# An input projection by eight blocks of plain products, and by seven products of one Strassen level in two sweeps of 1024 tokens

## The chip, the cores and the metric

The kernel runs on one core of a Trainium2 chip. The metric is the device time of one execution in microseconds (us). Engines: TensorE (PE, matrix products; PEld is its weight load), VectorE (DVE), ScalarE (ACT), GpSimd (POOL), and SyncE (SP), which here issues the transfers between DRAM and the on-chip memory SBUF. Products are summed up in PSUM.

## The reference

One layer on x of 2048 tokens by 1024 features. The input is normalised and modulated, multiplied by one wide matrix, and the columns of that product go two ways:

```python
mod = c_act @ w_ada[layer] + b_ada[layer]
shift, scale, gate = jnp.split(mod, 3, axis=-1)
h = rmsnorm(x, norm_g[layer]) * (1.0 + scale[:, None, :]) + shift[:, None, :]
proj = h @ w_in[layer]
u_f, z_f, q, k, v, r, gf_low, gb_low = jnp.split(proj, pts, axis=-1)
y_f = fourier_mix(u_f, w_fmap[layer]) * jax.nn.silu(z_f)
y_g = gla_mix(q, k, v, gf_low, gb_low, w_af[layer], b_af[layer],
              w_ab[layer], b_ab[layer], gla_norm_g[layer]) * jax.nn.silu(r)
y = jnp.concatenate([y_f, y_g], axis=-1) @ w_out[layer]
x = x + gate[:, None, :] * y
...
return rmsnorm(x, final_g)
```

`u`, `z`, `v` and `r` have 1024 columns each, `q` and `k` 512, the two gate inputs 16 each. `fourier_mix` is a two-dimensional Fourier transform over tokens and channels in four groups of 256 channels. `gla_mix` is gated linear attention with four heads, one scan over the tokens forward and one backward.

## The kernel before

**Three passes.** A float32 value is split into a high part (rounded by ACT) and a low part (the remainder, by DVE or POOL; `split`, L45). `mm3` (L49) makes a product of two split values from three matmuls: high by high, high by low, low by high. All large products are made so.

**Start.** x comes transposed, with features on partitions. Shift and scale come from `w_ada` (L202 to L308), and the modulated input is kept in SBUF as `hT`, high and low, in four blocks of 512 tokens. The first block of `u` is multiplied while the input is still being made.

**Projection.** The columns are worked off in blocks. `proj_tok` (L335) has tokens on the output's partitions: four blocks of 256 columns for `u`, four of 264 for `v`, with 24 matmuls of 256 or 264 columns for each of 16 token tiles. `proj_col` (L345) has columns on the output's partitions: four blocks of 256 for `z`, two for `q`, two for `k`, four for `r`, with 24 matmuls of 512 tokens for each of eight pieces. Weights are loaded and split for each block (`load_w`, L112). Products go to PSUM tiles `pj` (three buffers). `u` and `z` stay in SBUF (`U`, `Z`, with the SiLU of `z` taken on the way out of PSUM); q, k, v and r go to DRAM.

**Fourier group.** `fourier` (L476) runs four times. `stage1` (L377) is a 16-point transform along the tokens on DVE, in place in `U`. Then come five steps over pairs of frequencies: twiddle factors (`tw`, L492 to L495) and split (`gp`) on DVE and ACT, matmuls `pq` (L504), split (`PQ`, L505), matmuls `mapA` (L520 to L527), and the products with `Z` (L533 to L538). `U`, `Z`, `T` (which holds `tw` and `cm`), `gp` and `PQ` have one buffer each. The program text is u, z, Fourier of group g, then two of the blocks of q, k and v (L565 to L588), with the scaling of the output weights between.

**Linear attention.** First the gates are transposed (`gtr`, L622). The backward sweep goes over 8 blocks of 256 tokens and two pairs of heads: 16 half-blocks, each with `prework` (L640 to L701: decay logits `lg`, a scan on DVE, the decayed `Q` and `K`), scores `sc`, outputs `ob`, and for each half of 128 tokens a transpose of the keys `ktr`, a split and the state update `upd` (L715 to L734). Three blocks of `r` come next in the program text (L775), the last one after the first forward step (L814). Then the forward sweep makes the same again with the other gates, and the output projection `po` (L911) runs beside it.

**Order.** The program text gives dependences. A scheduler that simulates a timeline while the program is built decides the order of instructions on each engine, and this order is then fixed. An engine works its row in order, so an instruction that waits holds up all behind it.

Of the kernel before, what the change touches and what calls it, by code (L numbers as in the profile page):

```python
# [21 lines left out]
P = 128  # L22
L = 2048
# [3 lines left out]
WC = 264  # L27
EPS = 1e-6
# [6 lines left out]
def hybrid_kernel(ctx, tc, i, out):  # L35
    nc = tc.nc
    V, S, G, T = nc.vector, nc.scalar, nc.gpsimd, nc.tensor

# [6 lines left out]
    def split(hi, lo, src):  # L45
        S.activation(hi, src, AF.Copy)  # L46
        V.tensor_tensor(lo, src, hi.bitcast(F32), ALU.subtract)  # L47
# [14 lines left out]
    yd_ = dram.tile([P, 16, 8, P], F32, name="yf_d")  # L62
    gd_ = dram.tile([P, L], F32, name="g_d")
# [4 lines left out]
    od_ = dram.tile([16, 2, P, 512], F32, name="ob_d")  # L68

# [6 lines left out]
    mhalf = cp.tile([P, 4], F32, name="mhalf")  # L76
# [24 lines left out]
    def load_w_half(src, cols, h, pool=None):  # L101
        if pool is None:
            stg = sp.tile([P, 4, WC], F32, tag="wst", name="wst", bufs=1)
        else:
            stg = pool.tile([P, 4, 256], F32, tag="wst0", name="wst", bufs=2)
        load(stg[:, :, 0:cols], src[:, 4 * h:4 * h + 4, :])
        hi = wp.tile([P, 4, WC], F32R, tag="whi", name="whi")
        lo = wp.tile([P, 4, WC], F32R, tag="wlo", name="wlo")
        split(hi[:, :, 0:cols], lo[:, :, 0:cols], stg[:, :, 0:cols])
        return hi, lo  # L110

    def load_w(src, cols):  # L112
        return [load_w_half(src, cols, h) for h in range(2)]

    def stage_tile():
        return sp.tile([P, 512], F32, tag="st", name="st")

    def evac_q(blk, dst, scale, c, b, ps):
        s = stage_tile()
        S.activation(s[:], ps, AF.Copy, scale=scale)  # L120
        store(dst[:, 2 * b:2 * b + 2, 2 * (blk % 2) + c, :], s[:].rearrange("p (a t) -> p a t", a=2))

# [1 line left out]
    hT = []  # L124
    with ExitStack() as st_stack:
        st = st_stack.enter_context(tc.tile_pool(name="start", bufs=2))
        ccol = st.tile([P, KT], F32, name="ccol", bufs=1)
        bcol = st.tile([P, KT, 2], F32, name="bcol", bufs=1)
        ng = st.tile([P, KT], F32, name="ng", bufs=1)
# [5 lines left out]
        S.activation(cact[:], ccol[:], AF.Silu)  # L135

        def new_h(b):
            hT.append(tuple(big_tile(f"hT_{n}{b}")[:].rearrange("p (k t) -> p k t", k=KT) for n in ("hi", "lo")))
            return hT[b]

        def modulate(hi, lo, x, k, n):
            g_, s_ = gs[:, k:k + 1], shift[:, k:k + 1]
            if n != 512 and k in (1, 3, 5, 7):
                V.tensor_scalar(x, x, g_, s_, ALU.mult, ALU.add)  # L144
                V.tensor_copy(hi, x)
                V.tensor_tensor(lo, x, hi.bitcast(F32), ALU.subtract)
                return
            S.activation(hi, x, AF.Identity, bias=s_, scale=g_)  # L148
            if n == 512:
                rest = st.tile([P, 512], F32, tag="rest", name="rest")  # L150
                S.activation(rest[:], hi.bitcast(F32), AF.Identity, bias=s_, scale=-1.0)
                V.scalar_tensor_tensor(lo, x, g_, rest[:], ALU.mult, ALU.add)
            else:
                V.tensor_scalar(x, x, g_, s_, ALU.mult, ALU.add)
                V.tensor_tensor(lo, x, hi.bitcast(F32), ALU.subtract)  # L155
# [16 lines left out]
        def load_x(hb):
            b, o = hb // 2, (hb % 2) * 256
            xb = st.tile([P, KT, 256], F32, tag="xb", name="xb", bufs=2)
            load(xb[:], i["xT"][b][:, :, o:o + 256])
            return xb

        def bcast_rstd(pair):
            rb = pf.tile([P, 256], F32, tag="pq", name="rb", bufs=2)
            for t in range(2):  # L180
                T.matmul(rb[:, t * P:(t + 1) * P], pair[t][:, 0:1].to_broadcast([P, P]), ident[:],
                         start=True, stop=True)
            return rb

        xt = up.tile([P, KT, 512], F32, tag="U", name="xt")
        ada = [big_f32(f"ada{j}") for j in range(4)]
        fin = big_f32("fold_in")
        fout = big_f32("fold_out")
        tabs = fin[:, 0:1024].rearrange("p (k w) -> p k w", k=2)
        wf = fin[:, 1024:3072].rearrange("p (g k d) -> p g k d", g=NG, k=2)  # L190

        def ada_block(j):
            return ada[j // 2][:, (j % 2) * 2048:(j % 2 + 1) * 2048].rearrange("p (k w) -> p k w", k=KT)

        wst0 = []

        def load_wst(h):
            stg = st.tile([P, 4, 256], F32, tag="wst0", name="wst", bufs=2)
            load(stg[:], i["w_in"][0][:, 4 * h:4 * h + 4, :])
            wst0.append(stg)  # L200

        for n in range(2):  # L202
            load(xt[:, 4 * n:4 * n + 4], i["xT"][0][:, 4 * n:4 * n + 4])
        load(tabs, i["chtab"].rearrange("k p w -> p k w"))
        load(wf[:, 0:2], i["w_fmap"][0:2].rearrange("g (k p) d -> p g k d", p=P))
        load(wf[:, 2:4], i["w_fmap"][2:4].rearrange("g (k p) d -> p g k d", p=P))
        load(ada_block(0), i["w_ada"][0])
# [71 lines left out]
        for j in range(KT):  # L279
# [20 lines left out]
            if j == 2:  # L300
                split_wst(1)
# [725 lines left out]
```

## Time and profile before

| what | value |
|---|---|
| time of three runs | 1719.95, 1710.4, 1714.62 us; median 1714.62 us |
| span of the profiled execution | 1708.0 us |
| median less that span (launch and end, and what runs differ by) | 6.6 us |
| busy in the span: PE, DVE, ACT, POOL | 1642.6, 932.0, 596.9, 247.0 us |
| moved by the DMA engines | 213.60 MB, 125 GB/s on average |
| read from and written to DRAM | 145.65 MB, 66.32 MB |

The page of the profile gives the span but not the profiled execution's own device time; for this the median stands in. "xN" is a count, and `out<-in` names the tiles that an instruction writes and reads. In the window view each engine has its busy time and, in brackets, its instructions. PEclk is the granted clock of PE, 1.00 being full speed. A matmul's listed duration is longer than the step from one to the next, as they are pipelined; the pace is read from the count in a window.

### The profile page before, as it was taken

How to read it: one execution, taken by the hardware profiler on the slowest of the kernel's cores; microseconds unless marked ns; L12 is line 12 of the kernel's file. 1: busy time of each engine (PE TensorE's matmuls, PEld its weight loads, DVE VectorE, ACT ScalarE, POOL GpSimd, SP SyncE). 2: the span in 40 equal slices, each digit the busy share in tenths (PEclk: the TensorE clock that was granted, in tenths of full speed). 3: DMA queues.
4: the chain of work that ended last, by engine and by line, in shares of the span. 5: the costliest groups of instructions: out<-in, count | busy, mean ns of one | idle time of the engine just before them, and what ended most of it. 6: DMA issues, size and time to landing. Idle time of an engine off the chain costs nothing.

```text
span 1708.0 us, 24827 instructions
## 1 busy us (share of the span) xinstructions
PE 1642.6 (96%) x9632; PEld 1445.5 (85%) x9632; DVE 932.0 (55%) x1930; ACT 596.9 (35%) x1188; POOL 247.0 (14%) x239
## 2 busy tenths in 40 slices
PE   5879999999999999999999999998899999999997
PEld 4868888988889899998999888887778888888886
DVE  5687242262421544215351588889766576576562
ACT  3632221112211222122221355455554454454442
POOL 2250000110011000000000021235312122131220
PEclk9889999999999999999999999999999999999999
DMA  9541113531134112701124455567734434444331
GB/s 363 181 136 46 44 62 94 194 101 50 62 120 158 36 55 69 248 26 38 45 75 134 143 176 182 167 222 217 249 105 157 139 100 145 129 129 134 110 109 50
DMA packets 143383, 213.60 MB, mean 125 GB/s; under 512 B 12833, under 2 KB 95009, under 8 KB 141857
## 3 DMA queue, kind: packets, MB, share of 16 engines
q1 hardware_dynamic: 143120, 211.76, 38.4%
q8 instruction: 75, 1.23, 0.3%
q14 instruction: 44, 0.35, 0.1%
q10 hardware_dynamic: 144, 0.26, 0.0%
HBM read 145.65 MB, written 66.32 MB: 124 GB/s over the span
## 4 chain that ended last, share of the span: by engine, by line
PE 68%; issue 12%; DVE 8%; DMA 7%; POOL 3%; ACT 2%; SPq 0%; POOLq 0%; DVEq 0%; ACTq 0%
PE pj L54 45%; PE po L911 7%; PE mapA L54 3%; PE pq L54 3%; PE upd L54 2%; PE ob L767 1%; DMA v_d<-st 1%; PE fold L235 1%; DMA y<-yf_d 1%; PE sc L711 1%; DVE xb L144 1%; POOL vl L742 1%; POOL rstd L854 1%; PE cps L285 1%; PE sc L712 1%
## 5 line engine op out<-in xcount | busy, mean ns | idle before, releaser
L54 PE MATMUL pj<-hT_hi,whi 128*128 128x512 f32 x768 | 304.6, 397 | 0.1
L54 PE MATMUL pj<-hT_lo,whi 128*128 128x512 f32 x768 | 304.5, 396 | 0.0
L54 PE MATMUL pj<-hT_hi,wlo 128*128 128x512 f32 x768 | 304.2, 397 | 0.0
L54 PE MATMUL pj<-whi,hT_lo 128*128 128x264 f32 (+1 forms) x992 | 282.6, 286 | 12.0 <-DVE hT_lo L155 8.6
L54 PE MATMUL pj<-whi,hT_hi 128*128 128x264 f32 (+1 forms) x992 | 283.2, 286 | 1.9 <-ACT hT_hi L148 1.4
L54 PE MATMUL pj<-wlo,hT_hi 128*128 128x264 f32 (+1 forms) x992 | 283.2, 286 | 1.2 <-DVE wlo L47 1.2
L742 POOL TENSOR_TENSOR vl<-v,vh 128x512 fp32r<-128x512 f32 x64 | 95.0, 1485 | 768.0 <-DMA qi<-q_d 421.2
L54 PEld LDWEIGHTS pj<-whi,hT_lo 128*128 128x128 f32 x992 | 188.8, 191 | 13.4 <-DVE hT_lo L155 9.4
L54 PEld LDWEIGHTS pj<-whi,hT_hi 128*128 128x128 f32 x992 | 189.3, 191 | 3.2 <-ACT hT_hi L148 1.6
L54 PEld LDWEIGHTS pj<-wlo,hT_hi 128*128 128x128 f32 x992 | 189.9, 191 | 1.7 <-DVE wlo L47 1.4
L54 PEld LDWEIGHTS pj<-hT_hi,whi 128*128 128x128 f32 x768 | 144.4, 188 | 31.6 <-ACT U L546 0.5
L54 PEld LDWEIGHTS pj<-hT_hi,wlo 128*128 128x128 f32 x768 | 144.2, 188 | 31.5
L54 PEld LDWEIGHTS pj<-hT_lo,whi 128*128 128x128 f32 x768 | 144.5, 188 | 30.2
L47 DVE TENSOR_TENSOR wlo<-wst,whi 128x1024 fp32r<-128x1024 f32 (+1 forms) x38 | 46.8, 1232 | 169.2 <-ACT whi L46 169.1
L911 PE MATMUL po<-wo_hi,fhi 128*128 128x512 f32 x256 | 104.2, 407 | 8.3 <-ACT fhi L46 3.6
L911 PE MATMUL po<-wo_hi,ghi 128*128 128x512 f32 x256 | 103.0, 402 | 0.0
L911 PE MATMUL po<-wo_lo,fhi 128*128 128x512 f32 x256 | 102.6, 401 | 0.0
L911 PE MATMUL po<-wo_lo,ghi 128*128 128x512 f32 x256 | 102.3, 399 | 0.0
L911 PE MATMUL po<-wo_hi,flo 128*128 128x512 f32 x256 | 101.6, 404 | 0.5 <-DVE flo L47 0.4
L47 DVE TENSOR_TENSOR PQ<-pq,PQ 128x512 fp32r<-128x512 f32 x36 | 24.9, 692 | 125.7 <-ACT PQ L46 125.7
L911 PE MATMUL po<-wo_hi,glo 128*128 128x512 f32 x256 | 83.4, 401 | 0.2 <-DVE glo L47 0.2
L471 POOL TENSOR_TENSOR wos<-wos,gater 128x1024 f32<-128x1024 f32 x8 | 20.5, 2580 | 385.6 <-issue 209.2
(216 smaller groups left out, 3097.7 us busy)
## 6 DMA issues: line engine op xcount, KB each, us to landing
wst<-in_w_in SPq DMA_DIRECT2D x32, 512.0 KB, 4.5
v<-v_d SPq DMA_DIRECT2D x64, 256.0 KB, 2.9
xr<-in_x SPq DMA_DIRECT2D x28, 512.0 KB, 4.1
v_d<-st SPq DMA_DIRECT2D x64, 132.0 KB, 1.8
ada<-in_w_ada SPq DMA_DIRECT2D x8, 1024.0 KB, 16.0
yf_d<-Z SPq DMA_DIRECT2D x8, 1024.0 KB, 7.0
wos<-in_w_out SPq DMA_DIRECT2D x8, 1024.0 KB, 5.6
wo_d<-wos SPq DMA_DIRECT2D x8, 1024.0 KB, 4.9
```

The source lines that it names most:

```text
L47: V.tensor_tensor(lo, src, hi.bitcast(F32), ALU.subtract)
L54: T.matmul(ps, a, b, start=(k == 0), stop=(k == n - 1))
L144: V.tensor_scalar(x, x, g_, s_, ALU.mult, ALU.add)
L235: T.matmul(ps[:, ct, :], tabs[:, k, w * 256 + ct * P:w * 256 + (ct + 1) * P], wf[:, g, k, :], start=(k == 0), stop=(k == 1))
L285: T.matmul(cps[:, w:w + 1], wa[:, k, w * P:(w + 1) * P], cact[:, k:k + 1], start=(k == 0), stop=(k == KT - 1))
L471: G.tensor_tensor(w[:, a], w[:, a], g[:], ALU.mult)
L711: T.matmul(ps[:, h, 0:128], ki[:, c0:c0 + P], qi[:, c0:c0 + P], start=True, stop=True)
L712: T.matmul(ps[:, h, 128:192], K[:, g, kof:kof + P], Q[:, g, qof:qof + 64], start=True, stop=True)
L742: G.tensor_tensor(vl[:], v[:], vh[:].bitcast(F32), ALU.subtract)
L767: T.matmul(ob[:, h, :], pre[2][:, 2 * h + s, 64:192], st_b[hp][:, h, :], start=True, stop=True)
L854: G.tensor_tensor(r[:, 0:n], r[:, 0:n], mhalf[:, 0:n], ALU.pow)
L911: T.matmul(ps[h][:], a, wo[j][q][:, cs], start=(first and a is yh and q == 0), stop=(last and a is yl))
```

## The change

The features and the tokens of one sweep, and the columns of a block, are each halved, and the product of two 2 by 2 block matrices is made by seven products of sums in place of eight (Strassen's method in Winograd's form, once). A sweep has 1024 tokens; the second half of the tokens goes first (m = 1), then the first half (m = 0).

- `a_tiles`, `a_prep` (new): seven sums of the input for each of four pairs of feature blocks, split into high and low. SBUF holds the set of one sweep (14 tiles of 2048 columns).
- `b_prep` (new, first sweep): for each block of columns the sums of the weights (POOL) and seven split pieces; each piece is stored to DRAM (`bc_`, `bt_`). `b_load` (new, second sweep) loads them from there. Pieces lie in tiles `B`, six buffers.
- `block_col`, `block_tok` (new): seven products each, gathered by DVE in SBUF tiles `p1`, `u2`, `u3`, and stored. A block of 256 columns by `block_col` has 84 matmuls of 512 tokens in a sweep; one of 512 or 528 columns by `block_tok` has 336 matmuls of 256 or 264 columns.
- `u` and `z` go through DRAM too (`u_d`, `z_d`); `load_u` and `load_z` fetch them, with the SiLU of `z` there. The scaling of `q` moves into `prework`.
- The first sweep is all of z, u, v, q, k, r for tokens 1024 to 2047. The second sweep's blocks stand between the Fourier groups in the program text.
- `lg`, `gtr` and `ktr` share one PSUM buffer (tag `lt`); before, `lg` had its own (tag `lg`), and `gtr` and `ktr` shared another (tag `tr`) with the forward sweep's `otr`.

```diff
+    def x_scale(x, rb, eng):
+        for kk in range(2):
+            eng.tensor_tensor(x[:, kk], x[:, kk], rb[:, 0], ALU.mult)
...
+    ORDER = (1, 6, 7, 5, 2, 4, 3)
+    LOW = {1: G, 6: V, 7: G, 5: V, 2: G, 4: V, 3: G}
...
+            if k == 6:
+                t[1] = tmp("t1")
+                G.tensor_tensor(t[1], q[0, 1], q[0, 0], ALU.subtract)
+                G.tensor_tensor(q[0, 1], q[1, 1], q[0, 1], ALU.subtract)
+                G.tensor_tensor(q[0, 0], q[1, 1], t[1], ALU.subtract)
+                return q[0, 0]
...
+                t = b_tile()
+                bv = b_view(t, np_, n)
+                split(bv[:, 0], bv[:, 1], source(k, h), LOW[k])
+                store(dst[len(srcs) * order.index(k) + h][:, 0:2 * np_ * n], t[:, 0:2 * np_ * n].bitcast(F32))
...
+    def block_col(A, B, emit):
+        t1, u2, u3 = (tmp_t(name)[:, 0:512] for name in ("p1", "u2", "u3"))
+        for k in ORDER:
+            ps = pj_tile()
+            for p in range(4):
+                for q, (bq, aq) in enumerate(PASSES):
+                    T.matmul(ps[:], B[k][0][:, bq, p, :], A[k][aq][:, p, :], start=(p == 0 and q == 0),
+                             stop=(p == 3 and q == 2))
+
+            def add(o, a):
+                V.tensor_tensor(o, a, ps[:], ALU.add)
+            if k == 1:
+                S.activation(t1, ps[:], AF.Copy)
+            elif k == 6:
+                add(u2, t1)
+            elif k == 7:
+                add(u3, u2)
...
+    for g in range(4):
+        do_z(1, A, g)
+    with tc.tile_pool(name="tokraw", bufs=1, side="right") as tk:
+        for j in range(2):
+            do_u(1, A, j)
+        for j in range(2):
+            do_v(1, A, j)
...
+    do_u(0, A, 0)
+    do_z(0, A, 0)
+    fourier(0, load_u(0), load_z(0))
+    acc = gate_sums()
+    do_z(0, A, 1)
+    do_q(0, A, 8, qd_)
+    gate_row(acc)
+    scale_out_weights([0, 2])
+    fourier(1, load_u(1), load_z(1))
+    scale_out_weights([4, 6, 8])
+    do_u(0, A, 1)
+    do_z(0, A, 2)
+    do_q(0, A, 9, qd_)
+    fourier(2, load_u(2), load_z(2))
+    scale_out_weights([10, 12, 14])
+    do_z(0, A, 3)
+    do_q(0, A, 10, kd_)
+    fourier(3, load_u(3), load_z(3))
+    do_q(0, A, 11, kd_)
+    for j in range(2):
+        do_v(0, A, j)
...
-        lg = pg.tile([P, 512], F32, tag="lg", name="lg")
+        lg = pg.tile([P, 512], F32, tag="lt", name="lg")
...
-        tp = pg.tile([P, 512], F32, tag="tr", name="ktr")
+        tp = pg.tile([P, 512], F32, tag="lt", name="ktr")
...
     for blk in range(12, 15):
-        do_r(blk)
+        do_r(0, A, blk)
```

The order on PE at one place of the Fourier group: before, in the middle of a pair of a late group (`pj` are the projection's matmuls).

```order
L54 MATMUL pj<-whi,hT_hi_603 128x264
L54 MATMUL pj<-wlo,hT_hi_603 128x264
L54 MATMUL mapA<-PQ,wm 128x256 x2
L54 MATMUL pj<-whi,hT_lo_604 128x264
L54 MATMUL pj<-whi,hT_hi_603 128x264
L54 MATMUL pj<-wlo,hT_hi_603 128x264
L54 MATMUL pj<-whi,hT_lo_604 128x264
L54 MATMUL mapA<-PQ,wm 128x256 x22
```

After, on PE in the third Fourier group's first pair, these rows stand (A and B are the new sums).

```order
L260 MATMUL pj<-A_hi,B 128x512 x2
L260 MATMUL pj<-A_lo,B 128x512
L260 MATMUL pj<-A_hi,B 128x512
L56 MATMUL pq<-thi,gp 128x256
L56 MATMUL pq<-tlo,gp 128x256
L56 MATMUL pq<-thi,gp 128x256 x2
L56 MATMUL pq<-tlo,gp 128x256
L56 MATMUL pq<-thi,gp 128x256
L56 MATMUL mapA<-PQ,wm 128x256 x2
L56 MATMUL pq<-thi,gp 128x256
L56 MATMUL pq<-tlo,gp 128x256
L56 MATMUL mapA<-PQ,wm 128x256 x22
```

Its third row is the program's last `pj` matmul: all blocks of the second sweep, `v` and `r` among them, stand ahead of it, and behind it the rows of the third and fourth Fourier groups follow each other with no `pj` between.

The order on PE in the backward sweep: before, at one half-block's logits.

```order
L54 MATMUL pj<-hT_lo_604,whi 128x512
L54 MATMUL pj<-hT_hi_603,wlo 128x512
L54 MATMUL pj<-hT_hi_603,whi 128x512
L651 MATMUL lg<-gt,wabb 128x256 x2
L767 MATMUL ob<-state_8088,Q 128x256 x2
L54 MATMUL upd<-vh,kth 128x256
L54 MATMUL upd<-vl,kth 128x256
L711 MATMUL sc<-qi,ki 128x128
L54 MATMUL upd<-vh,ktl 128x256
```

After, on PE from the second key transpose of the first half-block.

```order
L805 MATMUL ktr<-ident,K 128x128 x2
L850 MATMUL ob<-state_9037,Q 128x256 x2
L56 MATMUL upd<-vh,kth 128x256
L56 MATMUL upd<-vl,kth 128x256
L56 MATMUL upd<-vh,ktl 128x256
L56 MATMUL upd<-vh,kth 128x256
L56 MATMUL upd<-vl,kth 128x256
L56 MATMUL upd<-vh,ktl 128x256
L734 MATMUL lg<-gt,wabb 128x256 x2
L794 MATMUL sc<-qi,ki 128x128
```

Before, a half-block's logits stand ahead of the last update of the half-block before it, with `pj` around both; now they stand behind that update, and nothing of another half-block or of the projection lies between them and the scores that need them.

The order on DVE in the backward sweep: before, around the state updates (L733) of one half-block.

```order
L659 SCALAR_TENSOR_TENSOR pa<-lg,pa 128x512
L733 SCALAR_TENSOR_TENSOR state_8088<-state_8088,sm,upd 128x256 x2
L663 SCALAR_TENSOR_TENSOR pb<-reset,pa 128x512
L762 COPY sb<-sc 64x2x64
L47 TENSOR_TENSOR ktl<-ktr,kth 128x256
L733 SCALAR_TENSOR_TENSOR state_8088<-state_8088,sm,upd 128x256 x2
L670 COPY sm<-pb 128x8
```

After, around the same updates (L816 now).

```order
L816 SCALAR_TENSOR_TENSOR state_9037<-state_9037,sm,upd 128x256 x2
L49 TENSOR_TENSOR ktl<-ktr,kth 128x256
L816 SCALAR_TENSOR_TENSOR state_9037<-state_9037,sm,upd 128x256 x2
L719 TENSOR_TENSOR gt<-gf,gt 32x256
L742 SCALAR_TENSOR_TENSOR pa<-lg,pa 128x512
L746 SCALAR_TENSOR_TENSOR pb<-reset,pa 128x512
```

Before, the next half-block's prework (`pa`, the scan `pb`) goes on between the two updates; now it begins after the second.

More of the change, by code (lines that the diff above doesn't have):

```diff
@@ L75, in hybrid_kernel @@
     cact = cp.tile([P, KT], F32, name="cact")
[L76 removed]
+    mhalf = cp.tile([P, 8], F32, name="mhalf")
     gcol = cp.tile([P, KT], F32, name="gcol")
@@ L99, in pj_tile @@
         return pj.tile([P, 512], F32, tag="pj", name="pj")
[L101 to L110, printed above, removed]
@@ L112, in load_w @@
-    def load_w(src, cols):
-        return [load_w_half(src, cols, h) for h in range(2)]
-    def stage_tile():
[L116 to L124, printed above, removed]
-    with ExitStack() as st_stack:
[L126 to L129, printed above, removed]
+    def stage_tile():
+        return sp.tile([P, 2 * WC], F32, tag="st", name="st", bufs=4)
@@ new lines, in weights @@
+    def weights(kind, b, m):
+        if kind == "col":
+            if not m:
+                return b_load(1, 4, 128, bc_[b], ORDER)
+            raw = rw.tile([P, 2 * BW], F32, tag="raw", name="raw", bufs=1)
+            return b_prep([i["w_in"][b + 4]], 4, 128, bc_[b], [raw], ORDER)
+        n_ = 256 if b < 2 else WC
+        if not m:
+            return b_load(2, 2, n_, bt_[b], TOK_ORDER)
+        src = i["w_u"][b] if b < 2 else i["w_v"][b - 2]
+        raws = [tk.tile([P, 2 * BW], F32, tag="traw", name="traw", bufs=2) for _ in range(2)]
+        return b_prep([src[:, 4 * h:4 * h + 4, :] for h in range(2)], 2, n_, bt_[b], raws, TOK_ORDER)
@@ L172, in load_x @@
[L172 to L207, printed above, removed]
-        load_wst(0)
-        load(ada_block(1), i["w_ada"][1])
-        load(ada_block(2), i["w_ada"][2])
-        load(ada_block(3), i["w_ada"][3])
@@ new lines, in hybrid_kernel @@
+    xstack.close()
+    for g in range(4):
[5 more added lines that the diff above has]
+            do_v(1, A, j)
+    xp = xstack.enter_context(tc.tile_pool(name="xs2", bufs=1, side="right"))
+    xs = x_tiles(0)
+    rb = x_rstd(0, xs)
+    for p in range(4):
+        x_scale(xs[p], rb, G)
+    for blk in (8, 9):
+        do_q(1, A, blk, qd_)
+    for blk in (10, 11):
+        do_q(1, A, blk, kd_)
@@ L375, in hybrid_kernel @@
+    for blk in range(12, 16):
+        do_r(1, A, blk)
+    A = a_tiles()
+    for p in range(4):
+        a_prep(A, p, xs[p], LOW)
+    xstack.close()
+    prep.close()
     fconst = {}
+    up = fstack.enter_context(tc.tile_pool(name="u", bufs=1))
+    fp = fstack.enter_context(tc.tile_pool(name="f", bufs=1))
     def stage1(U, h):
@@ new lines, in load_z @@
+        for c in range(2):
+            load(Z[:, c], zd_[:, 2 * g + c])
+            S.activation(Z[:, c], Z[:, c], AF.Silu)
+        return Z
+    thi = fp.tile([P, 640], F32R, name="thi")
+    tlo = fp.tile([P, 640], F32R, name="tlo")
+    tw = fp.tile([P, 8, 3], F32, name="tw")
+    tabstg = fp.tile([P, 640], F32, tag="T", name="tabstg")
+    load(tabstg[:], i["seqtab"])
+    load(tw[:], i["tw"])
+    split(thi[:], tlo[:], tabstg[:])
+    fconst.update(thi=thi, tlo=tlo, tw=tw)
+    do_u(0, A, 0)
@@ L874, in tail_fwd @@
                                 ALU.mult)
-            tp = pg.tile([P, 4, P], F32, tag="tr", name="otr")
+            tp = pt.tile([P, 4, P], F32, tag="tr", name="otr")
             for c in range(4):
```

511 lines of the change are left out of this document (268 added, 243 removed).

## The prediction

> **What bounds the kernel now.** I read the page first (busy time, slices), then the groups by line, then windows by stage, then single pieces of the timeline.
>
> ```profile
> span 1708.0 us, 24827 instructions
> PE 1642.6 (96%) x9632; PEld 1445.5 (85%) x9632; DVE 932.0 (55%) x1930; ACT 596.9 (35%) x1188; POOL 247.0 (14%) x239
> PE   5879999999999999999999999998899999999997
> ```
>
> PE bounds: 96% busy, and its slices are full from the fourth on. How many matmuls the projection has is in the groups; their listed means (397 and 286 ns) overlap, so the pace comes from windows.
>
> ```profile
> L54 PE MATMUL pj<-hT_hi,whi 128*128 128x512 f32 x768 | 304.6, 397 | 0.1
> L54 PE MATMUL pj<-whi,hT_lo 128*128 128x264 f32 (+1 forms) x992 | 282.6, 286 | 12.0 <-DVE hT_lo L155 8.6
> ...
> 0.00:43.00 43.00, 23.90 (x103) 21.34 (x103) 25.35 (x42) 14.74 (x22) 12.24 (x13) 0.91 0.93 363
> 560.00:590.00 30.00, 30.00 (x131) 24.21 (x130) 20.22 (x72) 4.93 (x9) 0.00 (x0) 1.00 0.11 35
> 817.00:860.00 43.00, 43.00 (x358) 43.00 (x357) 17.55 (x37) 9.83 (x22) 0.00 (x0) 1.00 0.10 32
> 953.60:1179.90 226.30, 225.62 (x1223) 193.34 (x1222) 187.77 (x353) 117.31 (x229) 55.46 (x35) 1.00 0.59 185
> 1179.90:1708.00 528.10, 503.35 (x2590) 420.76 (x2588) 337.85 (x670) 245.94 (x521) 120.73 (x150) 0.99 0.41 131
> 1190.00:1210.00 20.00, 12.58 (x52) 10.24 (x53) 15.09 (x30) 13.80 (x24) 4.88 (x4) 0.83 0.92 308
> ```
>
> From 560 to 590 us PE runs `pj` of 512 alone: 30/131 = 0.23 us each. From 817 to 860 it runs matmuls of 256 and 264: 43/358 = 0.120 us. The fourth window is the backward sweep, the fifth the forward sweep, as these rows of their logits bound them; the first row is the gate transpose:
>
> ```profile
> 926.27 0.60 PE L622 MATMUL gtr<-ident,g 128*96 128x128 f32 x4
> ...
> 953.60 0.40 PE L651 MATMUL lg<-gt,wabb 128*128 128x256 f32 x2
> ...
> 1179.89 0.28 PE L651 MATMUL lg<-gt,wabf 128*128 128x256 f32 x1
> ```
>
> The same windows for tile `pj` alone show what keeps PE full in the backward sweep:
>
> ```profile
> 953.60:1179.90 226.30, 162.78 (x642) 117.67 (x641) 17.74 (x26) 0.00 (x0) 1.00 0.59 185
> 1179.90:1708.00 528.10, 4.61 (x18) 3.20 (x17) 1.33 (x2) 0.00 (x0) 0.99 0.41 131
> ```
>
> So 162.8 of its 226.3 us are projection, and the sweep's own products take 62.8. The sweep is a chain of dependent steps, and the projection is the work that PE does while the chain runs elsewhere. The Fourier groups stand the same.
>
> **The change part by part.** *Matmuls.* Before, 3x768 = 2304 of 512 and 3x992 + 96 (in the start) = 3072 of 264: 2304x0.23 + 3072x0.12 = 899 us. After, 12 blocks x 2 sweeps x 84 = 2016 and 4x2x336 = 2688: 786 us. Off: 112 us of PE time. That is the gain if PE stays full.
>
> *What covers what.* The order on PE says it doesn't: the last `pj` stands in the third Fourier group's first pair. Behind it come the rest of that group, all of the fourth, and the backward sweep, with nothing to fill PE. I price these three by their chains.
>
> A Fourier pair, from DVE, ACT and PE in the middle of a group:
>
> ```profile
> 141.52 1.23 DVE L389 TENSOR_TENSOR T<-U 128x1024 f32<-128x1024 f32 x1
> ...
> 165.39 0.30 DVE L436 COPY U<-T 128x256 f32<-128x256 f32 x1
> ...
> 829.19 0.41 PE L54 MATMUL mapA<-PQ,wm 128*128 128x256 f32 x2
> ...
> 838.26 0.69 DVE L47 TENSOR_TENSOR gp<-tw,gp 128x512 fp32r<-128x512 f32 x1 [0.70 <-ACT gp L46]
> ...
> 840.21 0.28 PE L54 MATMUL pq<-thi,gp 128*128 128x256 f32 x1
> ...
> 843.68 0.68 DVE L47 TENSOR_TENSOR gp<-tw,gp 128x512 fp32r<-128x512 f32 x1
> ...
> 845.89 0.28 PE L54 MATMUL pq<-thi,gp 128*128 128x256 f32 x1
> ...
> 848.88 0.69 DVE L47 TENSOR_TENSOR PQ<-pq,PQ 128x512 fp32r<-128x512 f32 x1 [4.52 <-ACT PQ L46]
> ```
>
> From `mapA` to the `gp` that the first `pq` needs: 838.95 - 829.19 = 9.8 us. From that `pq` to the second one's `gp`: 844.36 - 840.21 = 4.2. From there to `PQ`: 849.57 - 845.89 = 3.7. With hand-overs 18 us for a pair when PE waits for nothing else (22 as it ran). A group has three such pairs, one of the kind without twiddles (half, 9) and one with a single frequency, whose products `mapA` still have to be taken to `Z` at the end (19, an estimate): 82, I take 80. `stage1` takes 24 us (first two rows, with three other instructions between).
> Third group uncovered: **80**. Fourth: `U` has one buffer, so its 2 MB load starts when the third is through; 512 KB of `wst` take 4.5 us (below) and the load is wider, so 8; `stage1` 26; `scale_out_weights` stands on DVE inside it, 8; pairs 80: **122**. Gate transpose to logits as before, 953.6 - 926.3 = **27**.
>
> The backward sweep's chain:
>
> ```profile
> 956.61 0.58 ACT L654 ACTIVATE pa<-lg 128x512 f32<-128x512 f32 x1
> 957.21 1.28 ACT L641 ACT_TABLE_LOAD   x1
> ...
> 967.55 0.42 DVE L701 TENSOR_TENSOR K<-K,sm 128x256 f32<-128x256 f32 x1
> ...
> 972.26 0.38 ACT L46 ACTIVATE kth<-ktr 128x256 fp32r<-128x256 f32 x1
> ...
> 975.00 0.42 DVE L47 TENSOR_TENSOR ktl<-ktr,kth 128x256 fp32r<-128x256 f32 x1
> ...
> 981.90 1.02 PE L767 MATMUL ob<-state,Q 128*128 128x256 f32 x4
> ...
> L733 DVE SCALAR_TENSOR_TENSOR state<-state,sm,upd 128x256 f32<-128x256 f32 x112 | 48.6, 474 | 24.6 <-PE upd L54 24.4
> ```
>
> Logits to `K`: 967.97 - 956.61, less the 1.28 of a table load, is 10.0 us. Then a transpose (0.4), `kth` 0.38, `ktl` 0.42, six `upd` (6x0.12 and the pipeline, 0.8), two state updates 0.95, `ob` 0.5, six `upd` 0.8, two updates 0.95, next logits 0.4: 5.6, with eight hand-overs some 6.2. Before, one half-block's 10 us ran while the other's updates ran, and 16 took 226.3, 14.1 each. After, `lg` shares one PSUM buffer with `ktr`, stands on PE behind the last `upd`, and on DVE the prework stands behind the second update: nothing overlaps. 16 x 16.2 = **259**. Bounds: 240 (15 each), 290 (18).
>
> *First sweep.* The window 0:43 moved 363 GB/s. The start now needs 4 MB of x, 1.5 MB of Fourier maps, 8 MB of `w_ada` and 1 MB of weights: 14.5 MB, 40 us, and the normalisation stands ready at 43. Then POOL is in the way:
>
> ```profile
> L742 POOL TENSOR_TENSOR vl<-v,vh 128x512 fp32r<-128x512 f32 x64 | 95.0, 1485 | 768.0 <-DMA qi<-q_d 421.2 <-ACT vh L741 346.8
> L330 POOL TENSOR_TENSOR xb<-xb,rbs 128x1024 f32<-128x1024 f32 x10 | 25.9, 2612 | 10.1 <-DMA xb<-in_xT 9.6 <-issue 0.5
> ...
> 26.65 8.94 DVE L266 SCALAR_TENSOR_TENSOR acc<-ada,cact,acc 128x256 f32<-128x256 f32 x7
> ...
> 37.27 3.61 DVE L266 SCALAR_TENSOR_TENSOR acc<-ada,cact,acc 128x256 f32<-128x256 f32 x7
> ...
> wst<-in_w_in SPq DMA_DIRECT2D x32, 512.0 KB, 4.5
> ```
>
> Eight multiplications of 1024 (`x_scale`) are 8x2.61 = 21, sixteen low parts of 512 are 16x1.49 = 24; with 7 of waits the first block can run at 95, and its last six products take 17: **112** (95 to 135). The remaining sweep is 11x84x0.23 + 4x336x0.12 = 374. A block also stores 3.7 MB of weight pieces, loads 1 MB and stores 1 MB: 5.7 MB in 19.3 us, 295 GB/s, under the 363 above, so hidden, but near it. POOL has 4 sums and 4 low parts per block, 8x1.49 = 11.9 of 19.3 us: hidden. Stalls: `x_scale` of the second half stands on POOL between weight sums, 21 us of which 13 show; two raw tiles of `w_v`, `w_u` loaded at each of four changes (3 each), and some at the others (8): 33. **407** (385 to 490).
>
> DVE beside POOL is slowed: seven accumulations took 8.94 us while POOL multiplied, 3.61 alone. DVE has 7 sums and 3 low parts of 0.69 in a block, 6.9 of 19.3 us, and even 2.5 times that is hidden. The Trainium skill, SBUF — State Buffer, section "SBUF: two separate sides", says that a DVE instruction with two SBUF inputs and a GpSimd one lock each other out for the whole instruction; by it DVE plus POOL, 6.9 + 11.9 = 18.8 of 19.3 us, would be nearly full in the first sweep; a slip there belongs to rival B.
>
> *Second sweep to the last `pj`.* 1008x0.23 + 1344x0.12 = 393, and 432 Fourier matmuls of the first two groups, 52; their order leaves about 16 us of `pj` between the steps of a pair against the 18 that its chain takes, 2 in each of six pairs: 12. **457** (440 to 480). Loads of pieces (3.7 MB a block, none to split) are hidden as above.
>
> *Forward sweep.* Its `pj` were 4.6 us: 528 - 5, less some waits that the separate `otr` buffer frees, **520** (500 to 530).
>
> *The clock.* With PE 63% busy (1190 to 1210) 0.83 was granted. On the uncovered chains PE's own steps are 2x26 (Fourier) and 16x3 us, 100; at 0.83 they cost **20** more.
>
> Sum: 112 + 407 + 457 + 80 + 122 + 27 + 259 + 20 + 520 = 2004 us. The median of before is 6.6 over its span; so **2010 us**, 17% slower: 112 us saved on PE, and some 410 in which it now waits where it did not (about 150 in two Fourier groups, 202 less their own 52; 215 in the backward sweep, 279 less 63; 27 at the gates; the rest in the start and the stalls).
>
> **The rivals.**
> A, the chains overlap down to what DVE has to do. Its rows in a Fourier pair:
>
> ```profile
> 834.93 0.63 DVE L537 TENSOR_TENSOR Z<-Z,cm 128x256 f32<-128x256 f32 x1
> 835.47 0.65 DVE L538 TENSOR_TENSOR Z<-Z,cm 128x256 f32<-128x256 f32 x1
> 836.16 0.35 DVE L492 TENSOR_SCALAR tw<-U,tw 128x256 f32<-128x256 f32 x1
> 836.69 0.48 DVE L494 SCALAR_TENSOR_TENSOR tw<-U,tw 128x256 f32<-128x256 f32 x1
> ```
>
> Two each of four `tw` (1.7), `gp` and `PQ` (1.4) and four steps on `cm` and `Z` (2.1, the first two 0.4 each) are 10.3 us by durations that overlap a little: 9.5 a pair, 41 a group; with `stage1` and 10 for load and scaling the fourth has 75. The backward sweep has 187.77 - 17.74 = 170. Without a clock loss: 112+407+457+41+75+27+181+515+7 = 1822. For: engines queue ahead, and before, the two half-blocks did overlap. Against: the order on DVE, and the shared buffer.
> B, the first sweep is fed too slowly (295 GB/s asked, or DVE and POOL locking each other out): 16 blocks x 5 us = 80 more, 2090. For: 0.93 DMA share at 363 GB/s. Against: large pieces.
> C, PE goes cold on the chains. At half clock its 100 us cost 100, not 20: 2090. The Trainium skill, TensorE: Matmul & The Clock Gate, Part 1, says that the granted clock falls to half after an idle window of about 3.4 us; the row with 0.83 at 63% busy agrees in direction only, so the row, not the rule, has the larger chance.
> D, faster: the second sweep's projection still covers the chains, PE stays the bound: 1715 - 112 = 1603, plus some start. It decides at a total of some 200 us for all stretches without `pj` (80+122+27+259 = 488 here): below that, the saved 112 win. DVE alone has 41+75+170 = 286 in them, which speaks against.
>
> **How the numbers follow.** Forecast 0.60; A 0.14; B 0.12; C 0.10; D 0.04, of it 0.03 faster and 0.01 the same. The range leaves out A and D (0.18): low from the low ends (95+385+440+70+100+20+240+500+7 = 1857), so 1860; high 2130, over B and C together with some of the high ends. A difference of 0.5% is about what a measurement of this kernel can tell from none: faster 0.03, same 0.01, slower 0.96.
>
> **What would show it.** Last `pj` near 976 us; PE busy about 75%; no `pj` behind it; logits 16 us apart, not 14; PE's granted clock under 1.00 in these stretches. It is wrong if PE's slices stay at 9 behind the last `pj`, if the half-blocks come every 11 us (A), if the first sweep ends beyond 600 us (B), or if the last `pj` stands later than 1100 us.

## The result, and the profile after

The changed kernel takes 2036.92 us in the median of four runs (2035.31 to 2042.27), against 1714.95 us of the kernel before on the same chip: 1.190 times as long (95% interval 1.186 to 1.194). The forecast was 2010 us in a range of 1860 to 2130.

Page of the changed kernel's profile, span, busy times and slices:

```profile
span 2035.8 us, 25168 instructions
...
PE 1654.2 (81%) x8984; PEld 1429.6 (70%) x8984; DVE 1118.3 (55%) x2196; ACT 624.8 (31%) x1182; POOL 490.3 (24%) x406
...
PE   6379999799899999999952543645558999999998
...
PEclk8679999899999999999965666666768999999999
```

PE has 648 matmuls fewer and is busy for longer, since a matmul at a low granted clock counts for longer (one of 512 columns 0.80 us at 0.50 in place of 0.40, below). The slices show two places: the second, with 3, and ten from the twenty-first on, where PE's digit falls to 2 to 6 and its clock to 0.5 to 0.7. Before, these eleven were 8 or 9.

Window view of the changed kernel by stage (PE, PEld, DVE, ACT, POOL busy with their instructions, granted clock, DMA share, GB/s). In order: start and first block of z; rest of z; u and v; q, k and r of the first sweep; second sweep to the last `pj`; the rest of the Fourier groups; gate transposes; backward sweep; forward sweep:

```profile
0.00:140.00 140.00, 70.79 (x308) 59.40 (x309) 83.93 (x114) 49.21 (x77) 66.51 (x42) 0.73 0.51 189
140.00:200.00 60.00, 56.99 (x244) 45.22 (x243) 21.93 (x30) 13.96 (x24) 38.05 (x30) 1.00 0.75 282
200.00:361.00 161.00, 160.16 (x1341) 159.95 (x1340) 60.92 (x113) 41.78 (x73) 72.64 (x56) 1.00 0.79 294
361.00:558.00 197.00, 176.36 (x763) 140.52 (x762) 85.58 (x104) 61.18 (x100) 125.86 (x84) 0.95 0.70 253
558.00:1014.00 456.00, 448.09 (x2741) 399.67 (x2742) 270.52 (x589) 64.31 (x105) 29.61 (x13) 0.99 0.81 284
1014.00:1202.00 188.00, 93.41 (x427) 81.28 (x425) 120.06 (x251) 41.19 (x65) 15.32 (x6) 0.63 0.30 107
1202.00:1225.00 23.00, 3.48 (x17) 2.07 (x16) 4.29 (x18) 3.06 (x6) 0.00 (x0) 0.57 0.57 171
1225.00:1519.00 294.00, 148.25 (x616) 122.16 (x616) 151.37 (x326) 114.77 (x227) 41.78 (x33) 0.65 0.33 107
1519.00:2036.00 517.00, 496.70 (x2536) 419.32 (x2536) 319.68 (x656) 235.35 (x506) 100.57 (x144) 0.97 0.38 123
```

Two bounds need care. The first sweep's last product ends at 551 us, so the last 7 us of the fourth window (some 60 matmuls) belong to the second sweep. The last bound is the first `po` matmul (1519); the forward sweep's first logits, which bound the windows of the prediction and most of those below (not e3's and e11's), come at 1535.9. By them the backward sweep takes 311 us and the forward sweep 500.

The second sweep to the last `pj` runs at PE's pace. Behind it come 188 + 23 + 294 = 505 us in which nothing bounds by its busy time: DVE, the busiest, has 276 of them. Such a stretch is a chain. The list of what PE waited for names its links (total, times, longest):

```profile
PE sc L794 <- DVE ki L763: 118.3, 16, 10.6
PE pq L56 <- ACT gp L48: 81.0, 14, 41.1
PE pj L260 <- POOL A_lo L49: 28.3, 4, 19.0
PE pj L260 <- ACT B L48: 25.4, 7, 13.8
```

The first is the prework of each of the 16 half-blocks. The second has two parts, as PE's timeline of the Fourier groups shows:

```profile
1049.66 5.75 PE L56 MATMUL mapA<-PQ,wm 128*128 128x256 f32 x24 [0.69 <-ACT PQ L48]
...
1068.29 5.06 PE L56 MATMUL mapA<-PQ,wm 128*128 128x256 f32 x24 [0.69 <-ACT PQ L48]
...
1128.34 0.58 PE L56 MATMUL pq<-thi,gp 128*128 128x256 f32 x1 [41.13 <-ACT gp L48]
```

One wait of 41 us is `stage1` of the fourth group, with the scaling of output weights between; the other 40 us are the twiddled values of the pairs, which come 18.6 us apart (first two rows). The last two entries of the list are mostly the start. PE's timeline in the backward sweep, logits and the scores behind them (last bracket: wait before it):

```profile
1247.20 0.40 PE L734 MATMUL lg<-gt,wabb 128*128 128x256 f32 x2
1255.15 0.79 PE L794 MATMUL sc<-qi,ki 128*128 128x128 f32 x2 [7.55 <-DVE ki L763]
...
1265.05 0.40 PE L734 MATMUL lg<-gt,wabb 128*128 128x256 f32 x2
1272.84 0.80 PE L794 MATMUL sc<-qi,ki 128*128 128x128 f32 x2 [7.39 <-DVE ki L763]
...
1284.86 0.40 PE L734 MATMUL lg<-gt,wabb 128*128 128x256 f32 x2
```

From logits to logits 17.9 and 19.8 us; over all 16, from 1225.2 to the last at 1510.8, 19.0. Each time PE stands still for 7.5 us for the keys of the very half-block whose logits it has just made.

### The profile page after: what moved, and what is told of

Same layout as the page of the kernel before. It is cut to its first block, busy times and chain, and to the rows that moved or that the text cites. A ratio compares the mean times of both kernels' runs of the same rounds, so it can differ in the third digit from the quotient of the medians.

```text
span 2035.8 us, 25168 instructions
## 1 busy us (share of the span) xinstructions
PE 1654.2 (81%) x8984; PEld 1429.6 (70%) x8984; DVE 1118.3 (55%) x2196; ACT 624.8 (31%) x1182; POOL 490.3 (24%) x406
## 5 line engine op out<-in xcount | busy, mean ns | idle before, releaser
L260 PE MATMUL pj<-A_hi,B 128*128 128x512 f32 x1344 | 438.0, 405 | 47.3 <-ACT B L48 25.4
L260 PEld LDWEIGHTS pj<-A_hi,B 128*128 128x128 f32 x1344 | 257.8, 193 | 115.5 <-ACT B L48 29.5
L303 PE MATMUL pj<-B,A_hi 128*128 128x256 f32 (+1 forms) x1792 | 326.3, 283 | 4.0 <-DVE u L264 2.4
L260 PE MATMUL pj<-A_lo,B 128*128 128x512 f32 x672 | 271.6, 404 | 28.3 <-POOL A_lo L49 28.3
L303 PEld LDWEIGHTS pj<-B,A_hi 128*128 128x128 f32 x1792 | 278.4, 189 | 4.9 <-DVE u L264 2.6
L303 PE MATMUL pj<-B,A_lo 128*128 128x256 f32 (+1 forms) x896 | 253.4, 283 | 0.8 <-DVE A_lo L49 0.8
L794 PE MATMUL sc<-qi,ki 128*128 128x128 f32 x256 | 72.6, 375 | 124.7 <-DVE ki L763 118.3
L260 PEld LDWEIGHTS pj<-A_lo,B 128*128 128x128 f32 x672 | 129.5, 193 | 60.8 <-POOL A_lo L49 30.7
L303 PEld LDWEIGHTS pj<-B,A_lo 128*128 128x128 f32 x896 | 169.1, 189 | 1.0 <-DVE A_lo L49 1.0
L56 PE MATMUL mapA<-PQ,wm 128*128 128x256 f32 x480 | 80.0, 327 | 7.9 <-ACT PQ L48 6.2
```

The source lines that it names most:

```text
L56: T.matmul(ps, a, b, start=(k == 0), stop=(k == n - 1))
L260: T.matmul(ps[:], B[k][0][:, bq, p, :], A[k][aq][:, p, :], start=(p == 0 and q == 0), stop=(p == 3 and q == 2))
L303: T.matmul(ps[:, j, :], A[k][aq][:, p, t * P:(t + 1) * P], B[k][p // 2][:, bq, p % 2, :], start=(p == 0 and q == 0), stop=(p == 3 and q == 2))
L794: T.matmul(ps[:, h, 0:128], ki[:, c0:c0 + P], qi[:, c0:c0 + P], start=True, stop=True)
```

## The experiments

Each was timed in several runs beside the kernel before, which took 1710 to 1715 us. "Ratio" is to that kernel, with its 95% interval.

| run | us | ratio |
|---|---|---|
| changed kernel | 2036.9 | 1.190 (1.186 to 1.194) |
| e1: before, r moved ahead | 1806.2 | 1.055 (1.051 to 1.058) |
| e8: before, shared buffer | 1841.5 | 1.073 (1.069 to 1.077) |
| e11: before, both of these | 1941.8 | 1.136 (1.133 to 1.138) |
| e2: changed, logits' own buffer | 1911.6 | 1.116 (1.113 to 1.119) |
| e3: changed, r late | 2033.7 | 1.187 (1.183 to 1.190) |
| e4: changed, PE kept busy | 2000.2 | 1.167 (1.163 to 1.170) |
| e5: changed, start on VectorE and spread | 2034.1 | 1.186 (1.182 to 1.189) |
| e6: e2, e3 and e5 together | 1923.2 | 1.121 (1.118 to 1.124) |
| e7: e6 and Fourier buffers | 1812.3 | 1.057 (1.053 to 1.061) |
| e9: e2 and Fourier buffers | 1812.5 | 1.058 (1.056 to 1.061) |
| e10: e9 and the start on VectorE | 1790.2 | 1.045 (1.043 to 1.046) |

**The cover alone (e1).** In the kernel before, with plain products, the four blocks of r join the first Fourier group's list and leave the backward sweep:

```diff
-    others = [[lambda: do_q(8, qd_, P ** -0.5), lambda: do_q(9, qd_, P ** -0.5)],
+    others = [[lambda: do_q(8, qd_, P ** -0.5), lambda: do_q(9, qd_, P ** -0.5)] +
+              [lambda blk=blk: do_r(blk) for blk in range(12, 16)],
...
-    for blk in range(12, 15):
-        do_r(blk)
...
-    do_r(15)
```

> The kernel before, plain products, with its four blocks of r moved from the backward sweep into the first Fourier group; nothing of the change is in it. Theory (cover): time is lost where chains run with no projection beside them, whatever the products cost. Then 4x192x0.23 = 177 us are spent earlier, and the backward sweep, which took 226 us with them, takes some 200 without: 1715 + 177 - 26 = 1866 us (1835 to 1910). Rival (the loss lies in the new products themselves, their sums and trips through DRAM): moving plain products about costs nothing, 1715 within 15.

It took 1806, 93 us more: slower without any Strassen product, but less than the 151 that I expected. The window of its backward sweep:

```profile
1124.00:1290.00 166.00, 117.53 (x628) 97.81 (x629) 154.29 (x328) 113.07 (x231) 45.70 (x32) 0.86 0.60 191
```

The sweep takes 166 us, not 200, and DVE is busy for 154 of them: without cover the half-blocks still overlap and VectorE sets the pace, 9.6 us each. Before, the same took 14.1, because the projection was there to be done. So lost cover does not explain 294 us in the changed kernel.

**The shared buffer (e2, e8, e11).** e2 gives the logits back their own PSUM buffer in the changed kernel, with the layout of before:

```diff
-    pj = ph1.enter_context(tc.tile_pool(name="pj", bufs=4, space=PSUM, side="right"))
+    pj = ph1.enter_context(tc.tile_pool(name="pj", bufs=3, space=PSUM, side="right"))
...
-            ps = pg.tile([P, 512], F32, tag="lt", name="gtr")
+            ps = pg.tile([P, 512], F32, tag="tr", name="gtr")
...
-        lg = pg.tile([P, 512], F32, tag="lt", name="lg")
+        lg = pg.tile([P, 512], F32, tag="lg", name="lg")
...
-        tp = pg.tile([P, 512], F32, tag="lt", name="ktr")
+        tp = pg.tile([P, 512], F32, tag="tr", name="ktr")
...
-            tp = pt.tile([P, 4, P], F32, tag="tr", name="otr")
+            tp = pg.tile([P, 4, P], F32, tag="tr", name="otr")
```

> The changed kernel with the PSUM layout of before: the logits have a buffer of their own, the key transposes share theirs with the forward sweep's transposes, three projection buffers in place of four. Theory (half-blocks of the backward sweep can't overlap because logits and key transposes share a buffer): they overlap again, 14 us each, 294 us become 225 to 240, and the time falls from 2037 to about 1975. Rival (each half-block's chain, lengthened by the low clock, sets the pace, whatever buffer it has): within 15 of 2037.

125 us less, twice what the theory gave. Its windows, Fourier rest, gates and backward sweep:

```profile
1019.00:1207.00 188.00, 90.48 (x428) 78.53 (x427) 120.24 (x251) 41.38 (x66) 15.31 (x6) 0.65 0.31 108
1207.00:1230.00 23.00, 4.12 (x17) 2.59 (x18) 4.23 (x17) 2.90 (x6) 0.00 (x0) 0.53 0.59 176
1230.00:1390.00 160.00, 112.47 (x631) 91.94 (x631) 149.12 (x323) 109.88 (x225) 44.65 (x31) 0.90 0.60 194
```

The other two stretches are as they were; the backward sweep falls from 311 to 160 by the same bounds, with the same work on DVE. Logits now start before the half-block ahead of them is through, as PE's timeline of this run shows, five in a row 7.6 to 11.8 us apart:

```profile
1244.73 0.78 PE L734 MATMUL lg<-gt,wabb 128*128 128x256 f32 x2
...
1252.35 0.48 PE L734 MATMUL lg<-gt,wabb 128*128 128x256 f32 x2
...
1264.14 0.50 PE L734 MATMUL lg<-gt,wabb 128*128 128x256 f32 x2 [1.21 <-DVE pa L742]
...
1274.56 0.58 PE L734 MATMUL lg<-gt,wabb 128*128 128x256 f32 x2
...
1284.39 0.58 PE L734 MATMUL lg<-gt,wabb 128*128 128x256 f32 x2
```

e8 is the mirror: the kernel before with `tag="lt"` for `lg`, `gtr` and `ktr`.

> The kernel before with one edit of the change: logits, gate and key transposes share one PSUM buffer. Its order on PE puts 23 us of projection into each of the first seven half-blocks and none into the last eight. Theory (the shared buffer makes every half-block one chain): seven of 23 + 4 us and nine of 16.5 are 338 in place of 226, and what is no longer spread must be paid: 1715 becomes 1770 to 1830. Rival (the chain of a half-block hides beside the projection): within 8 of 1715.

126 us more, in a kernel with plain products and all of its cover; that is above the 1830 at which the expectation ended. Its order packs the projection into the first half of the sweep (655 `pj` matmuls there, 6 in the second half), and the windows of the two halves show it:

```profile
953.50:1139.00 185.50, 183.71 (x901) 153.26 (x900) 96.79 (x170) 59.86 (x107) 31.49 (x19) 1.00 0.47 146
1139.00:1335.00 196.00, 110.35 (x449) 90.70 (x447) 104.19 (x211) 77.38 (x148) 31.49 (x22) 0.67 0.37 117
```

In the first half PE is full, in the second it has only the sweep's own matmuls at a clock of 0.67, and the 196 us are chain. e11 puts both edits into the kernel before.

> The kernel before, plain products, with both edits that were made to it singly: r moved into the first Fourier group, and logits and key transposes in one PSUM buffer. No Strassen product, no second sweep, no trip of weights through DRAM is in it. Theory (the shared buffer makes an uncovered half-block one chain of 18 to 19 us, as in the changed kernel): the backward sweep takes about 294 in place of 166, 1806 + 128 = 1934 (1915 to 1950). Rival (its length in the changed kernel comes from something else of the change, such as traffic or GpSimd's and VectorE's load): within 20 of 1806.

1942, as the theory said. Its backward sweep:

```profile
1124.00:1418.00 294.00, 147.37 (x618) 121.61 (x618) 151.87 (x327) 115.79 (x230) 42.70 (x33) 0.67 0.34 107
```

294 us to the first `po` with 618 matmuls at 0.67, where the changed kernel has 294 with 616 at 0.65; in both the logits come 19.0 us apart. Nothing of Strassen's method is in this run, so its traffic and its sums have no part in the sweep's length.

**The clock (e4).** Behind the logits of each half-block 36 matmuls into a spare buffer that nobody reads, and the blocks of r ahead of the sweep in the text, where their order on PE already was:

```diff
-            T.matmul(lg[:, h * 256:(h + 1) * 256], wab[d][:, c0:c0 + P], gt[:], start=True, stop=True)
+            mm = T.matmul(lg[:, h * 256:(h + 1) * 256], wab[d][:, c0:c0 + P], gt[:], start=True, stop=True)
+        if d == 1:
+            with tc.issue_after(mm.ins):
+                spare = pj_tile()
+                for n in range(36):
+                    T.matmul(spare[:], wab[1][:, 0:P], wab[1][:], start=(n == 0), stop=(n == 35))
```

> The changed kernel with 36 extra matmuls of 512 behind each half-block's logits in the backward sweep, into a spare buffer that nobody reads: 8.3 us at full clock in a wait of 7.5 to 10.6, and 17 x 8.3 = 141 us of PE work more. Theory (the low granted clock, 0.65 there, lengthens the steps of PE on the chain): the clock goes up to 0.9 or more and the backward sweep falls from 294 to about 260, the time to about 2003. Rival (the chain's other engines set the pace, and the clock costs only what PE would wait anyway): within 15 of 2037. If the extra work itself delays the scores: slower, 2050 or more.

37 us less for more work. Its backward sweep:

```profile
1228.00:1493.00 265.00, 234.88 (x1220) 196.88 (x1221) 154.46 (x337) 114.37 (x231) 42.70 (x33) 0.97 0.38 119
```

The granted clock is 0.97 in place of 0.65, and to the forward sweep's first logits the sweep takes 265 in place of 311. Half-blocks come every 16.7 us in place of 19.0; sixteen times 2.3 are the 37. With e2 this gives the parts: the chain at nearly full clock some 265, a low clock some 40 on top, and overlap would take 100 off (e2's 160).

**Cover moved within the changed kernel (e3, e6).** e3 makes `block_col` a generator that stops after each product, and takes two products of r behind each half-block's logits:

```diff
+        if d == 1:
+            with tc.issue_after(mm.ins):
+                next(rest, None)
+                next(rest, None)
...
-    for blk in range(12, 15):
-        do_r(0, A, blk)
+    for _ in rest:
+        pass
...
-    do_r(0, A, 15)
```

> The changed kernel with the second sweep's four blocks of r (28 products, 77 us) taken out from between the Fourier groups and put two by two behind the logits of the backward sweep's half-blocks, 5.5 us into a wait of 7.5 to 10.6. Theory (cover): they fill idle time there, the second sweep ends 50 to 77 us earlier, the backward sweep stays at 294 or gets shorter by a faster clock: 1935 to 1990. Rival (they were needed as cover between the Fourier groups, where as much waiting opens): within 15 of 2037.

No gain that can be told from none. Its windows, from the end of v to the gates, and the backward sweep:

```profile
940.00:1165.00 225.00, 96.02 (x432) 84.08 (x432) 135.40 (x322) 36.76 (x61) 9.37 (x4) 0.60 0.32 111
1187.00:1530.00 343.00, 247.71 (x1006) 201.14 (x1007) 196.27 (x376) 136.92 (x256) 63.15 (x41) 0.73 0.52 166
```

The gates start at 1166 in place of 1203, 37 us sooner for 77 us of matmuls taken away: the rest reappears as waiting. The backward sweep then takes up the 37: its half-blocks are 21.4 us apart in place of 19.0. The theory counted the products as free in a wait of 7.5 us, and they weren't; whether by the low clock or by their 28 additions on DVE this run doesn't separate. e6 tried the same with the logits' own buffer and e5's start.

> The changed kernel with three of the edits together: logits in a buffer of their own, r put late into the backward sweep, the start's multiplication on VectorE. From 1911 (logits alone) less 30 (start); r late saved 39 us ahead of the gates and gave them back in the backward sweep. Theory (given back because each half-block was one chain of 19 us): with overlapping half-blocks of 9.5 us the two products cost little, 1911 - 30 - 39 + 20 = 1862. Rival (given back whatever the buffer, by VectorE's additions and PE's order): 1880 or more.

1923, no better than e2 alone (1911.6). Its backward sweep takes 220 us, PE busy for 187 of them: the products fill it, and cost the 60 us that it is longer than e2's 160. The theory was wrong; cover is worth only what PE would wait for, and with overlap that is little.

```profile
1182.00:1402.00 220.00, 187.38 (x971) 156.57 (x972) 192.83 (x360) 124.60 (x243) 61.20 (x39) 0.92 0.76 247
```

**The Fourier chain (e7, e9).** Two buffers for `gp`, one of its own for `cm`, with two staging buffers in place of four to make room:

```diff
-                gp = fp.tile([P, 2, 2, 256], F32R, tag="gp", name="gp")
+                gp = fp.tile([P, 2, 2, 256], F32R, tag="gp", name="gp", bufs=2)
...
-                cm = fp.tile([P, 4, 2, P], F32, tag="T", name="cm")
+                cm = fp.tile([P, 3, 2, P], F32, tag="cm", name="cm")
...
-        return sp.tile([P, 2 * WC], F32, tag="st", name="st", bufs=4)
+        return sp.tile([P, 2 * WC], F32, tag="st", name="st", bufs=2)
```

> The kernel of the run before it, with two buffers for the split twiddled values of the Fourier step (gp) and a buffer of its own for cm, which shared one with the twiddle products; two staging buffers in place of four make room. Theory (the uncovered Fourier pairs are one chain of 18 us because of single buffers): 18 becomes 11 to 13, two groups save some 50 us. Rival (VectorE's work or the order sets the pair, not the buffers): within 10 of the run before it.

> The changed kernel with the logits' own buffer and the two buffers for gp and own buffer for cm, r and the start as the change has them. Theory (buffers made both uncovered chains long, and each of the two edits takes its own part): 1911 less the 111 that the Fourier buffers took off in the run of four edits = 1800 (1785 to 1815). Rival (the 111 came from r having left the Fourier groups): above 1850.

e7 took 111 us off e6, twice what was expected, and e9 99 off e2. That e7 and e9 are alike fits that the place of r is worth nothing (e7 also has e5's start). Window of e9 from the last `pj` to the gates:

```profile
1049.50:1108.00 58.50, 35.50 (x206) 32.76 (x205) 54.38 (x86) 21.55 (x34) 15.84 (x7) 0.80 0.35 119
```

58 us in place of 188. With shorter chains the whole third group runs beside the projection, so the last `pj` comes 36 us later than in the changed kernel, and only the pairs of the fourth are left; DVE is busy in 54 of their 58 us.

**The start (e5, e10).** e5 moves the multiplication of the first half of x by its norm from POOL to DVE (`x_scale(xs[p], rb, V)`) and spreads that of the second half over the blocks of q and k in the text.

> The changed kernel with the multiplication of the first half of x by its norm on VectorE in place of GpSimd, and that of the second half spread behind the four blocks of q and k. Theory (GpSimd's queue makes the start and the first q block late): the first block ends at about 120 in place of 140 us, the first q block takes 24 in place of 40, the time falls from 2037 to about 2005 (1995 to 2020). Rival (VectorE, 45 of 50 us busy there, becomes late in its place): within 10 of 2037.

Nothing that can be told from none (2034). The first Fourier group began 4 us sooner and no more: the first q block still took 40 us, from 356 to 396, as the scheduler put all eight multiplications together again (18.8 us in a row on POOL, from 370.4). e10 builds on e9, with both multiplications and all low parts of the first half's sums on DVE.

```diff
-                x_scale(xs[p], rb, G)
-                a_prep(A, p, xs[p], LOW)
+                x_scale(xs[p], rb, V)
+                a_prep(A, p, xs[p], {n: V for n in range(1, 8)})
...
-        x_scale(xs[p], rb, G)
+        x_scale(xs[p], rb, V)
```

> The kernel of the run before it with the start's low parts and both multiplications of x by its norm on VectorE, so that GpSimd's first work is the first block's weight sums. Theory (the weight sums behind the low parts made the start late, 31 us of waiting in the first block, and the multiplication of the second half cost the first q block 18): the first block ends at 115 in place of 140, the first q block takes 22 to 25 in place of 40, 35 to 40 us less than the run before it. Rival (the scheduler's order or VectorE takes it back later, as in the other start edit): within 10 of the run before it.

22 us less, some 60% of what was expected: the first block ends near 120, but the first q block still takes 38. POOL now has none of the input's work ahead of the first block's weight sums, and they are late all the same:

```profile
92.03 3.45 POOL L216 TENSOR_TENSOR t<-raw 128x512 f32<-128x512 f32 x1 [31.04 <-DVE A_lo L49]
```

The first sum `t` waits 31 us for DVE's low parts of the input. In the source the input's sums and `t` take turns in the same three buffers (tag `X`), so this may again be buffers and not a queue; no run varied them. With everything, 1790 us is 4.5% slower than before. What is left: 58 + 22 us behind the last `pj`, a backward sweep of 165 with 121 of PE, and in the first sweep a start of 120 and q, k and r in 195 us where 155 would do at PE's pace. No version here beats the kernel before.

## Why the prediction was right, point by point

- **The saving of PE time.** Right. The second sweep to the last `pj` took 463 us (from 551) against 457 forecast; u and v of the first sweep took 161, as worked out.
- **What covers what.** Right as read from the order: no `pj` behind the third group's first pair. The Fourier groups, the gates and the backward sweep behind it took 188, 23 and 311 us, by the bounds of the forecast's own windows, where 202, 27 and 279 (259 and the clock's 20) were forecast.
- **The start.** Too small: the first block ended at 137 us, not 112. The step had the normalisation ready at 43; POOL's first multiplication by the norm began at 60.5. Its input `ms` was there at 24, but the transposes that spread it (`rbp`) stand on PE behind the Fourier maps' and the shift's products, which keep PE busy until then. The 51 us that POOL then took are those of the forecast (52). Not counted either were the first block's own weight sums behind them. POOL's and PE's timelines:

```profile
22.43 1.83 POOL L139 TENSOR_TENSOR ms<-ms,mhalf 128x8 f32<-128x8 f32 x1 [22.00 <-DVE ms L138]
...
57.08 1.14 PE L143 MATMUL rbp<-ident,ms 128*128 128x128 f32 x8
...
60.49 20.72 POOL L150 TENSOR_TENSOR xs<-xs,ssum 128x1024 f32<-128x1024 f32 x8 [36.23 <-ACT ssum L145]
...
112.44 1.26 POOL L216 TENSOR_TENSOR t<-raw 128x512 f32<-128x512 f32 x1 [1.29 <-DVE A_lo L49]
...
118.08 0.80 PE L260 MATMUL pj<-A_hi,B 128*128 128x512 f32 x1 [13.81 <-ACT B L48]
```

  The first sum `t` runs at 112.4, the pieces made from it are ready at 118, and six products at half clock and full clock follow. So some 17 us of the miss are the late norm, which no run moved (`rbp` ran at 54 to 57 us in e5 and e10 too), and some 8 the sums and the low clock. The rest of the first sweep took 414 (137 to 551) against 407.
- **The clock.** Mis-sized: 20 us were forecast for all three stretches, at a clock of 0.83. It was 0.57 to 0.65 there, and e4 gave 37 us back, all in the backward sweep's half-blocks. Rival C's mechanism is real: at half clock it has 48 us for the sweep's own 16 x 3, and 37 were lost. What the clock cost in the Fourier groups no run shows.
- **The backward sweep.** Its chain was priced well, for a reason that is two things in one. At a clock of 0.97 (e4) it took 265 us and 16.7 a half-block, against 259 and 16.2; the rest of the 311 is for the most part the clock. The text named the lost cover, the shared buffer and the order together. e1 and e2 separate them: without cover but with its own buffer the sweep takes 160 to 166 us, less than the 226 of before, and the shared buffer adds some 144 to 150 (310 in e11 against 166, 311 against 160), of which the whole runs show 136 and 125. The step "nothing overlaps" holds only with the buffer; rival A's floor by DVE, 170 us, is about what the sweep would have run at.
- **The Fourier groups.** Right in size (188 against 202), in part by luck: the pairs' 18 us were worked out from rows at full clock, and the 18.6 measured hold a clock of 0.63, so the chain itself was priced somewhat too long. The wait ahead of the fourth group's pairs was 41 us where 42 (load, `stage1`, scaling) were forecast. e9 shows that the chain of 18 us is one of single buffers, which the text gave as links of a chain without saying that they could be broken.
- **Rival B.** It did not come: the first sweep ended at 551, not beyond 600, and u and v ran at PE's pace while 294 GB/s were moved.
- **Rival D.** Its break-even, some 200 us of stretches without `pj`, holds (1715 less 7 and the 1496 us of the forecast's other terms is 212). e10 has 58 + 22 + 165 = 245 there, 33 too many, and 1544 in the rest, 48 more than the 1496; it is 76 us slower than before.
- **The total.** That it came within 27 us is partly luck. The start (25), the rest of the first sweep (7), the second sweep (6) and the backward sweep with its clock (32) took more than forecast; the Fourier groups (14), the gates (4) and the forward sweep (20, 500 against 520) took less.
- **The signs.** The last `pj` came at 1014 us (976 forecast), half-blocks 19.0 us apart (16), and PE was busy 81% (75%), since its slow matmuls count for longer.

What the numbers add up to: of the 322 us by which the change is slower, 125 go when the logits get their own buffer (e2), 99 more with the Fourier buffers (e9), 22 more with the start (e10), and 76 are left.

## What to carry to other kernels

Before you save work on the engine that bounds, list the chains that this work covers, and look in the order of the built program where it now runs: work done early covers nothing later. Where cover goes, single buffers can become the bound (e9), and the shared PSUM buffer cost about as much with cover (126 us, e8) as without (136, e11 against e1); so ask of each single buffer which two steps it forces into one row. An order made by a simulated timeline follows the buffers as well; one shared PSUM buffer changed the order of a whole sweep (e8).

## What the runs showed of the hardware

The granted clock fell to 0.50 from 65 to 115 us, where PE had 12 matmuls, and one of 512 took 0.80 us in place of 0.40. The Trainium skill, TensorE: Matmul & The Clock Gate, Part 1, says that it falls to half after an idle window of about 3.4 us; this stretch agrees, with waits of 19.0 and 5.1 us, and so do the waits of 7.5 us in the backward sweep, where it is 0.65 on average.

DVE beside POOL in the start, timeline of the changed kernel; the last row stands where POOL had just paused:

```profile
83.36 1.75 DVE L171 TENSOR_TENSOR xs<-xs 128x512 f32<-128x512 f32 x1
85.03 1.76 DVE L175 TENSOR_TENSOR s<-s,xs 128x512 f32<-128x512 f32 x1
...
105.86 0.68 DVE L170 TENSOR_TENSOR s<-xs 128x512 f32<-128x512 f32 x1
```

The same instruction takes 1.75 us beside POOL's low parts (seven in 11.78 us, 1.68 each, from 82.85 us) and 0.68 without them: the two engines went in step, one instruction each. The Trainium skill, SBUF — State Buffer, section "SBUF: two separate sides", says of a VectorE instruction with two SBUF inputs and a GpSimd one that one waits for all of the other; the trace agrees, and the price in the start was 45 us of DVE for some 20 us of work.
